# Reciprocal norms by way of DRAM, and a new order of the first tiles, in a two-layer hybrid decoder trunk

## The chip, the cores and the metric

The kernel runs on one core of one Trainium2 chip. The metric is the device time of one execution in microseconds, taken as the median of several runs; a profiled execution of the same program gives the trace. All times below are microseconds unless they say otherwise.

## The reference

A residual stream of 528 tokens (16 meta tokens and 512 of the sequence) with d = 1024 passes two layers. Each is one sub-layer with two token mixers side by side:

```
h = RMSNorm(x)
u, z, c_q, c_kv, k_rope, z_mla, g_pool, g_mla = split(h @ W_in)
y_pool = (pool_mix(u) * silu(z)) @ W_pool_up
y_mla  = (mla(c_q, c_kv, k_rope) * silu(z_mla)) @ W_mla_up
x = x + (sigmoid(g_pool) * y_pool + sigmoid(g_mla) * y_mla) @ W_out
```

pool_mix takes running means over windows of 2, 4, 8 and 16 tokens in four channel groups and multiplies each by a matrix of its own. mla is attention with 8 heads: a query latent of 768 and a key-value latent of 256 channels are normed (RMSNorm) and projected up, queries and keys are normed again, a part of each is rotated by position, and the attention is causal. What matters here are two of the norms: the RMSNorm of x, and that of the key-value latent.

## The kernel before

**Layout.** Channels lie on the 128 partitions and tokens along the free dimension. x is held as eight slices of 128 channels. Every large product is done as three fp32r products (L179 to L182): each operand is split into a high and a low part, and hi·hi, hi·lo and lo·hi are added up in PSUM. A slice of x becomes its hi and lo part in split_h (L329); a weight block of 128 by 512 is loaded by SP into one of three raw buffers, copied to its high part by ScalarE (L175), and VectorE subtracts to get the low part (L176).

**The norms come after the products.** h is not divided by its norm ahead of the product with W_in; the scale is put on when a result is taken out of PSUM. For that the kernel needs 1/rms per token, repeated on all 128 partitions: self.inv (tag rinv) for x, and self.cinv for the key-value latent. norm_sums (L340) makes them in each layer. It sums the squares (L338 for x, L407 for the latent) with matmuls against ones (L348), copies the sums out (L355), transposes them so that tokens lie on partitions (L360, L361), and VectorE takes the reciprocal root by Newton steps (L283 to L290) in the small tile ny, 128 x 2 x 5. Then the way back begins. ny is split into a high and a low part in a tile of 170 columns (L372 to L378). rows() (L387) transposes it with five matmuls to four rows over the tokens, and ScalarE copies them to kinv (L394, L395). spread() (L273) multiplies kinv by a matrix of ones and zeros, two matmuls for each of the two results, which leaves a row on all partitions; ScalarE copies it out (L277). The values v take the reciprocal norm straight from ny, per partition (L582, L583).

**The order.** plan is a list of products (Gemm objects), and stream() (L187) is a generator that emits them in that order, weight loads four blocks ahead. The code in go() (L977) draws from it by step(), by upto(name), which runs until a product is done, and by fill_now(ns), which emits products worth so many nanoseconds; between these stands the other work: norm sums, mixing stages, heads. Within that, a scheduler orders each engine's instructions. Accumulators of these products come from four PSUM banks (mm) with one bank per half of the tokens, so that a product whose evacuation is late holds up the second product behind it.

**The start of the plan.** ckv0 and ckv1 (key-value latent), three of the six query-latent tiles cq0 to cq2, then u0, k0, u1, the rotary key kr, k1, u2, k2, u3, k3 (pooling input and keys by turns), cq3, v, the gates zp with the group products y, cq4 and cq5 among them, and then the queries. The evacuation of u, kr, the keys, zp and the later gates reads self.inv or self.cinv; that of ckv and cq doesn't. The sine and cosine tables (L292) come after u0, mixing stage 3 after cq3.

**The start of the kernel.** Ten matmuls on a tile of ones (L138) run while the first loads are under way. The first weight block is loaded on ScalarE's queue into the tile later used as rinv; on SP follow the gains gn, the slices of x (1, 1, 2, 2, 2), three raw blocks between them, the constants cst and the positions, all without a wait. In layer 0 go() emits split_h for the eight slices with four steps of the stream between, then ckv1, then the squares of the slices.

The existing precedent of a way through DRAM is that of the keys' norms: kdr is written by one DMA (L685) and read back as broadcasts (L694).

Of the kernel before, what the change touches and what calls it, by code (L numbers as in the profile page):

```python
# [54 lines left out]
LAG = 2000.0  # L55
BATCH = 8
SPL = 240
WARM = 10


def cut(v, bits):
# [10 lines left out]
def trunk(ctx, tc, xT, pos, win, wkr, wqb, wkb, wvb, wgr, wpu, wmu, wout, gains, const, yT):  # L72
# [26 lines left out]
    def mmt():  # L99
        return pp.tile([P, 512], F32, tag="mm", name=nm("mm"), bufs=4)  # L100
# [19 lines left out]
    early.append(fetch(win[0, MT_CKV, :, 0:512], 512, slot("rinv"), act))  # L120
    sp.dma_start(gn, gains)
    for k0, k1, m, c in ((0, 1, 1, 0), (1, 2, None, 0), (2, 4, 0, 1), (4, 6, 1, 1), (6, 8, None, 0)):
        sp.dma_start(xb[:, k0:k1, :T], xT[:, k0:k1, :])
        if m is not None:
            early.append(fetch(win[0, MT_CKV + m, :, 512 * c:512 * c + 512], 512, rawt(), sp))
    xt = [xb[:, k] for k in range(8)]
    sp.dma_start(cst, const)
# [4 lines left out]
    sp.dma_start(posb[:, :T], pos.partition_broadcast(P))  # L132
    ident = cst[:, C_ID:C_ID + P]
    ones = cp.tile([P, P], F32, name="ones")
    dve.memset(ones, 1.0)
# [2 lines left out]
        pe.matmul(wps[:, 0:P], ones, ones, start=True, stop=True)  # L138
    maskw = cp.tile([P, 512], BF16, name="maskw")
    gp.memset(maskw[:, :512 - P], 0.0)  # L140
    dve.tensor_copy(maskw[:, 512 - P:], cst[:, C_MASK:C_MASK + P])
    kinv = cp.tile([34, T], F32R, name="kinv")
    sel = cp.tile([64, 2], F32R, name="sel")
    gp.memset(sel.bitcast(F32), 0.0)
    for i in range(2):
        gp.memset(sel[32 * i:32 * i + 2, i:i + 1].bitcast(F32), 1.0)
    identr = cp.tile([P, P], F32R, name="identr")
    dve.tensor_copy(identr, ident)
# [30 lines left out]
    def mm3(out, wh, wl, xh, xl, start, stop):  # L179
        pe.matmul(out, wh, xh, start=start, stop=False)  # L180
        pe.matmul(out, wh, xl, start=False, stop=False)  # L181
        pe.matmul(out, wl, xh, start=False, stop=stop)  # L182

    plan = []
    done = set()

# [77 lines left out]
    def fill_now(ns):  # L264
        end = clk[0] + ns
        while clk[0] < end and step():
            pass
# [5 lines left out]
    def spread(dst, i):  # L273
        for a, b in FULL:
            ps = mmt()[:, :b - a]
            pe.matmul(ps, sel[0:34, i:i + 1].to_broadcast([34, P]), kinv[:, a:b], start=True, stop=True)
            act.activation(dst[:, a:b], ps, AF.Copy)  # L277

    def behind(ins, other):
        tc.add_manual_dep(ins.ins, other.ins.name,  # L280
                          mybir.DependencyInfo(mybir.DependencyClass.Sync, mybir.DependencyReason.DATA))
# [22 lines left out]
        dve.tensor_scalar(tcos, tcos, -2.0, 1.0, op0=ALU.mult, op1=ALU.add)  # L304

    scr = dp.tile([P, 8, SEQ], F32, name="scr")
    kdr = [[dp.tile([4, T], F32, name=f"kdr{l}{s}") for s in range(2)] for l in range(DEPTH)]

    hbuf = [(slot(f"hh{k}", F32R), slot(f"hl{k}", F32R)) for k in range(8)]

    class Layer:
        def __init__(self, l):
            self.l, self.last = l, l == DEPTH - 1
            self.XS = XTOK if self.last else FULL
            self.x0 = NM if self.last else 0
            self.xt = xt if l == 0 else [None] * 8
            self.hs, self.us, self.zps = hbuf, [None] * 4, [None] * 4
            self.cs, self.cqs, self.ys, self.am = [None] * 2, [None] * 6, [None] * 4, [None] * 8
            self.kn, self.qn, self.zms, self.ogs = [None] * 4, [None] * 4, [None] * 4, [None] * 4
            self.qr, self.qf = [None] * 2, [None] * 2  # L320
            self.gms, self.mg, self.xr, self.vw = [None] * 8, [None] * 8, [None] * 8, []
            self.csq, self.xsq = [None] * 2, [None] * 8
            self.sq, self.nsq, self.asq = [], [0, 0], 0
            self.st = self.acc = self.inv = self.cinv = self.kraw = self.kp = None
# [4 lines left out]
        def split_h(self, k):  # L329
            gk, x = self.g(G_H + k), self.xt[k]  # L330
            hh, hl = self.hs[k]
            act.activation(hh[:, :T], x[:, :T], AF.Copy, scale=gk)
            dve.scalar_tensor_tensor(out=hl[:, :T], in0=x[:, :T], scalar=gk, in1=hh[:, :T].bitcast(F32),
                                     op0=ALU.mult, op1=ALU.subtract)

        def square_x(self, k):
            self.xsq[k] = slot(f"cq{4 + k}" if k < 4 else f"q{k}")
            act.activation(self.xsq[k][:, :T], self.xt[k][:, :T], AF.Square)  # L338

        def norm_sums(self):  # L340
            fill_now(2600)
            ps = [mmt(), mmt()]
            for t, r, start, stop in [(self.xsq[k], 0, k == 0, k == 7) for k in range(6)] + [
                    (self.csq[0], 32, True, False), (self.xsq[6], 0, False, False),
                    (self.xsq[7], 0, False, True), (self.csq[1], 32, False, True)]:
                for s, (a, b) in enumerate(FULL):
                    r_ = r + 64 * s
                    mm = pe.matmul(ps[s][r_:r_ + 32, :HALF], ones[:, 0:32], t[:, a:b], start=start, stop=stop,  # L348
                                   tile_position=(0, r_))
                    if t is not self.csq[1]:  # L350
# [20 lines left out]
            w = tmp()  # L371
            gp.memset(w[:, 0:170], 0.0)  # L372
            v = w[:, 0:170].rearrange("p (j c) -> p j c", c=34)
            nv = ny.rearrange("p a j -> p j a")
            nh = sm.tile([P, 5, 2], F32R, tag="nh", name=nm("nh"))
            dve.tensor_copy(nh, nv)
            dve.tensor_copy(v[:, :, 0:33:32], nh.bitcast(F32))
            dve.tensor_sub(v[:, :, 1:34:32], nv, nh.bitcast(F32))  # L378
            fill_now(8200)
            self.rows(v, 34, kinv)  # L380
            self.inv, self.cinv = slot("rinv"), slot("cq9")
            fill_now(1300)
            spread(self.inv, 0)
            spread(self.cinv, 1)
            self.st = [sct(), sct()]

        def rows(self, v, n, out):  # L387
# [523 lines left out]
        def register(self, nxt):  # L911
# [14 lines left out]
            def kk(p):  # L926
                add(f"k{p}", wkb[l, p], 256, evac=self.ev_k(p), xs=cs, segs=FULL)

            for m in range(3):
                cq(m)  # L930
            for m in range(4):
                add(f"u{m}", wi(MT_U + m), D, evac=self.ev_u(m), xs=hs, segs=FULL)
# [6 lines left out]
            def y(m):  # L939
                add(f"y{m}", wgr[l, m], P, evac=self.ev_y(m), xs=lambda: [self.ys[m]], segs=XS)  # L940

            cq(3)
            add("v", wvb[l], 1024, body=self.v_body)
            zp(0)
            zp(1)
# [2 lines left out]
            y(1)  # L948
            zp(3)
            y(2)  # L950
            cq(4)
            y(3)
            cq(5)
            for r in range(2):
                add(f"qr{r}", wqb[l, r], 768, evac=self.ev_qr(r), xs=lambda: self.cqs, segs=XS)
            for p in range(4):
# [20 lines left out]
        def go(self, nxt):  # L977
            l = self.l
            up = lambda name: upto((l, name))
            if l == 0:  # L980
                for k in range(8):
                    if k in (0, 1, 3, 5):
                        step()
                    self.split_h(k)
            up("ckv1")
            if l == 0:
                for k in range(8):
                    self.square_x(k)
            self.norm_sums()
            up("u0")  # L990
            if l == 0:
                tables()
            up("u1")
# [1 line left out]
            self.mix(1)  # L995
            up("u3")
            self.mix(2)
            up("cq3")
            self.mix(3)
            up("qr1")  # L1000
            for s, (a, b) in enumerate(FULL):
# [109 lines left out]
```

## Time and profile before

| | us |
|---|---|
| median of three runs | 802.42 (802.06 to 803.46) |
| profiled execution | 803.0 |
| its span in the trace | 801.2 |

The page of the profile lists busy time per engine, the chain of work that ended last, and groups of instructions by line. In a timeline row stand the start, the length, the engine, the line, the operation with its tiles and shapes, the count, and in brackets the idle time ahead of it with what ended it. A matmul's length is longer than its distance to the next, since matmuls overlap; what one costs is read from start to start. Every fp32 matmul leaves several records, every fp32r product of 264 columns one. In the window view each row gives the stretch, its length, then busy time and count for each engine, the clock that TensorE was granted, and the DMA engines' busy share and rate. A row of landing times gives the size in KB and the median time from issue to landing.

### The profile page before, as it was taken

How to read it: one execution, taken by the hardware profiler on the slowest of the kernel's cores; microseconds unless marked ns; L12 is line 12 of the kernel's file. 1: busy time of each engine (PE TensorE's matmuls, PEld its weight loads, DVE VectorE, ACT ScalarE, POOL GpSimd, SP SyncE). 2: the span in 40 equal slices, each digit the busy share in tenths (PEclk: the TensorE clock that was granted, in tenths of full speed). 3: DMA queues.
4: the chain of work that ended last, by engine and by line, in shares of the span. 5: the costliest groups of instructions: out<-in, count | busy, mean ns of one | idle time of the engine just before them, and what ended most of it. 6: DMA issues, size and time to landing. Idle time of an engine off the chain costs nothing.

```text
span 801.2 us, 14644 instructions
## 1 busy us (share of the span) xinstructions
PE 793.5 (99%) x5343; PEld 715.1 (89%) x5343; DVE 527.8 (66%) x1139; ACT 417.0 (52%) x946; POOL 196.2 (24%) x266
## 2 busy tenths in 40 slices
PE   9999999999999999999999999999999999999998
PEld 8889999999999999999997897877788888887887
DVE  5568767437689887685354686665467889664942
ACT  7455645545556665543254456445455666644421
POOL 1024404103433322142000164032024333410600
PEclk9999999999999999999999999999999999999999
DMA  6222233324222222224642222324242322222272
GB/s 240 73 64 96 73 100 91 109 83 140 86 87 87 78 69 67 83 89 143 181 142 73 73 87 86 98 81 119 85 157 90 101 84 79 68 78 69 92 227 102
DMA packets 48872, 80.71 MB, mean 101 GB/s; under 512 B 5904, under 2 KB 14480, under 8 KB 48800
## 3 DMA queue, kind: packets, MB, share of 16 engines
q1 hardware_dynamic: 48656, 79.52, 32.3%
q8 instruction: 42, 0.69, 0.4%
q14 instruction: 30, 0.25, 0.1%
q10 hardware_dynamic: 144, 0.26, 0.1%
HBM read 73.40 MB, written 4.23 MB: 97 GB/s over the span
## 4 chain that ended last, share of the span: by engine, by line
PE 95%; DMA 2%; ACT 1%; DVE 1%; issue 0%; POOL 0%; SPq 0%; ACTq 0%; POOLq 0%
PE mm L180 28%; PE mm L182 27%; PE mm L181 27%; PE mm L798 2%; PE S L180 2%; PE S L181 2%; PE S L182 2%; PE o L804 1%; PE o L803 1%; PE mm L348 1%; PE S L457 1%; DMA raw<-wmu 1%; DMA xb<-xT 1%; DMA bc<-kdr 1%; PE mm L415 0%
## 5 line engine op out<-in xcount | busy, mean ns | idle before, releaser
L180 PE MATMUL mm<-hh,whi 128*128 128x264 f32 (+2 forms) x1096 | 346.3, 318 | 0.2 <-ACT racc L812 0.2
L181 PE MATMUL mm<-hl,whi 128*128 128x264 f32 (+2 forms) x1096 | 343.5, 314 | 0.0
L182 PE MATMUL mm<-hh,wlo 128*128 128x264 f32 (+2 forms) x1096 | 342.2, 315 | 0.0
L176 DVE TENSOR_TENSOR wlo<-raw,whi 128x512 fp32r<-128x512 f32 (+2 forms) x251 | 186.5, 747 | 120.1 <-ACT whi L175 112.6
L175 ACT ACTIVATE whi<-raw 128x512 fp32r<-128x512 f32 (+2 forms) x251 | 150.3, 602 | 185.9 <-PE mm L181 131.5
L180 PEld LDWEIGHTS mm<-hh,whi 128*128 128x128 f32 x1096 | 205.7, 188 | 13.5 <-ACT racc L812 0.5
L181 PEld LDWEIGHTS mm<-hl,whi 128*128 128x128 f32 x1096 | 206.2, 188 | 12.2 <-issue 0.4
L182 PEld LDWEIGHTS mm<-hh,wlo 128*128 128x128 f32 x1096 | 205.1, 188 | 12.7 <-issue 0.4
L704 POOL TENSOR_TENSOR tmp<-kp,bc 64x528 f32<-64x528 f32 x16 | 24.5, 1531 | 113.5 <-DMA bc<-kdr 78.2
L535 POOL TENSOR_TENSOR racc<-racc,tmp 128x264 f32<-128x264 f32 (+1 forms) x15 | 14.1, 942 | 143.5 <-ACT tmp L534 143.4
L776 POOL TENSOR_TENSOR pm<-pa,rs 128x16 f32<-128x16 f32 x32 | 11.6, 361 | 145.5 <-DVE rs L771 140.7
L886 POOL TENSOR_TENSOR tmp<-tmp,xb 128x264 f32<-128x264 f32 (+1 forms) x24 | 27.0, 1145 | 59.1 <-DVE tmp L884 33.7
L732 DVE CUSTOM_DVE_ANT_0 S<-S,maskw,nqs 128x272 f32<-128x272 f32 (+4 forms) x80 | 38.4, 498 | 1.6 <-PE S L182 1.2
L739 ACT ACTIVATE cq<-S,bia 128x400 f32<-128x400 f32 (+2 forms) x48 | 24.6, 516 | 21.5 <-DVE bia L766 11.6
L180 PE MATMUL mm<-u,whi 128*128 128x264 f32 (+1 forms) x108 | 35.3, 327 | 0.0
L182 PE MATMUL mm<-cq,wlo 128*128 128x264 f32 (+1 forms) x108 | 34.8, 323 | 0.0
L182 PE MATMUL mm<-u,wlo 128*128 128x264 f32 (+1 forms) x108 | 34.8, 322 | 0.0
L181 PE MATMUL mm<-cq,whi 128*128 128x264 f32 (+1 forms) x108 | 34.8, 322 | 0.0
L180 PE MATMUL mm<-cq,whi 128*128 128x264 f32 (+1 forms) x108 | 34.7, 322 | 0.0
L271 DVE TENSOR_TENSOR tl<-mm,th 128x512 fp32r<-128x512 f32 (+1 forms) x64 | 29.3, 481 | 6.8 <-ACT th L270 5.8
L778 POOL TENSOR_TENSOR cq<-cq,rs 128x384 f32<-128x384 f32 (+1 forms) x32 | 32.8, 1025 | 0.0
L180 PE MATMUL mm<-q,whi 128*128 128x264 f32 (+1 forms) x96 | 30.0, 324 | 1.0 <-ACT whi L175 0.5
(262 smaller groups left out, 1380.0 us busy)
## 6 DMA issues: line engine op xcount, KB each, us to landing
raw<-win SPq DMA_DIRECT2D x143, 256.0 KB, 2.6
raw<-wout SPq DMA_DIRECT2D x32, 256.0 KB, 3.1
bc<-kdr SPq DMA_DIRECT2D x16, 264.0 KB, 3.6
raw<-wpu SPq DMA_DIRECT2D x16, 256.0 KB, 2.7
raw<-wmu SPq DMA_DIRECT2D x16, 256.0 KB, 2.6
raw<-wqb SPq DMA_DIRECT2D x12, 256.0 KB, 2.7
tmp<-xT SPq DMA_DIRECT2D x16, 132.0 KB, 2.9
tmp<-scr SPq DMA_DIRECT2D x7, 256.0 KB, 4.7
```

Of the source, the lines that this page charges most:

```text
L175: act.activation(hi[:, :n], raw[:, :n], AF.Copy)
L176: dve.tensor_sub(lo[:, :n], raw[:, :n], hi[:, :n].bitcast(F32))
L180: pe.matmul(out, wh, xh, start=start, stop=False)
L181: pe.matmul(out, wh, xl, start=False, stop=False)
L182: pe.matmul(out, wl, xh, start=False, stop=stop)
L271: dve.tensor_sub(lo[:, a:b], src, hi[:, a:b].bitcast(F32))
L704: gp.tensor_mul(kf[r0:r0 + 64, :], self.kp[r0:r0 + 64, :], bc[r0:r0 + 64, :])
L732: dve.tensor_tensor_reduce(out=sv, in0=sv, in1=mask, scale=nqs[:, i, h:h + 1], scalar=3e38, op0=ALU.add, op1=ALU.min, accum_out=bia[:, c:c ...
L739: act.activation(pv, sv, AF.Exp, scale=-1.0, bias=bia[:, i:i + 1], accum_out=rs[:, c:c + 1])
L778: gp.tensor_mul(pt[i][:, NM:], pt[i][:, NM:], rs[:, i:i + 1].to_broadcast([P, n - NM]))
L798: pe.transpose(tr[:, P * (i - j):P * (i - j + 1)], pt[i][:, NM + P * j:NM + P * (j + 1)], ident)
L886: gp.tensor_add(t[:, :b - a], t[:, :b - a], self.am[m][:, a:b])
```

## The change

- **Norms.** The high-low split, rows() and spread() are no longer called for these norms, and kinv and sel are gone. ny is written to two DRAM rows by four DMAs on SP per layer: for each of the two norms one of 128 x 4 single elements, and one for the 16 meta tokens. After a stretch of products worth RET = 12500 nanoseconds, two DMAs on SP read each row back, broadcast to all partitions, into rinv and into q1 (before: cq9). These reads wait for the latest lo·hi product emitted up to there.
- **Order of the plan.** Five query-latent tiles come after ckv1 instead of three; cq3 before v and cq4 after y2 are gone from there, and cq5 comes after y2.
- **Other work.** In layer 0 the tables come right after norm_sums, in both layers mixing stage 3 comes after k3.
- **Start.** Five loads go first: the first weight block (ScalarE's queue), then gn, x0, one raw block and x1 on SP. All other early loads wait until the first weight block has landed. Eight warm-up matmuls instead of ten. The first slice is split in two halves of the tokens, and the square of slice k in layer 0 waits for the split of slice k + 3 (at most 7).

```
-WARM = 10
+RET = 12500.0
+WARM = 8
...
+    early.append(slot("rinv"))
+    first = act.dma_start(early[0][:, 0:512], win[0, MT_CKV, :, 0:512])
     sp.dma_start(gn, gains)
...
+    sp.dma_start(xb[:, 0, :T], xT[:, 0, :])
+    early.append(fetch(win[0, MT_CKV + 1, :, 0:512], 512, rawt(), sp))
+    sp.dma_start(xb[:, 1, :T], xT[:, 1, :])
...
+    def other_loads(made):
+        for k, m in ((2, 0), (4, 1), (6, None)):
+            ins = sp.dma_start(xb[:, k:k + 2, :T], xT[:, k:k + 2, :])
+            behind(ins, made)
+            if m is not None:
+                raw = rawt()
+                behind(sp.dma_start(raw, win[0, MT_CKV + m, :, 512:1024]), made)
+                early.append(raw)
+        behind(sp.dma_start(cst, const), made)
+        behind(sp.dma_start(posb[:, :T], pos.partition_broadcast(P)), made)
...
-        pe.matmul(out, wl, xh, start=False, stop=stop)
+        newest[0] = pe.matmul(out, wl, xh, start=False, stop=stop)
...
+            for a, b in FULL if (self.l, k) == (0, 0) else [(0, T)]:
+                made = act.activation(hh[:, a:b], x[:, a:b], AF.Copy, scale=gk)
+                self.made[k] = self.made[k] or made
...
+            made = act.activation(self.xsq[k][:, :T], self.xt[k][:, :T], AF.Square)
+            if self.l == 0:
+                behind(made, self.made[min(k + 3, 7)])
...
-            fill_now(8200)
-            self.rows(v, 34, kinv)
-            self.inv, self.cinv = slot("rinv"), slot("cq9")
-            fill_now(1300)
-            spread(self.inv, 0)
-            spread(self.cinv, 1)
+            self.inv, self.cinv = slot("rinv"), slot("q1")
+            for i, d in enumerate((self.inv, self.cinv)):
+                row = ndr[self.l][i]
+                sp.dma_start(row[0, NM:T].rearrange("(j p) -> p j", p=P), ny[:, i, 0:4])
+                sp.dma_start(row[0, 0:NM].rearrange("(p j) -> p j", j=1), ny[0:NM, i, 4:5])
+            fill_now(RET)
+            for i, d in enumerate((self.inv, self.cinv)):
+                behind(sp.dma_start(d[:, 0:T], ndr[self.l][i].partition_broadcast(P)), newest[0])
...
-            for m in range(3):
+            for m in range(5):
                 cq(m)
...
-            cq(3)
             add("v", wvb[l], 1024, body=self.v_body)
...
-            cq(4)
+            cq(5)
             y(3)
-            cq(5)
...
             self.norm_sums()
-            up("u0")
             if l == 0:
                 tables()
...
-            up("cq3")
+            up("k3")
             self.mix(3)
```

More of the change, by code (lines that the diff above doesn't have):

```diff
@@ L118, in rawt @@
         return wp.tile([P, 512], F32, tag="raw", name=nm("raw"), bufs=3)
-    early.append(fetch(win[0, MT_CKV, :, 0:512], 512, slot("rinv"), act))
+    early.append(slot("rinv"))
+    first = act.dma_start(early[0][:, 0:512], win[0, MT_CKV, :, 0:512])
     sp.dma_start(gn, gains)
[L122 to L125, printed above, removed]
+    sp.dma_start(xb[:, 0, :T], xT[:, 0, :])
+    early.append(fetch(win[0, MT_CKV + 1, :, 0:512], 512, rawt(), sp))
+    sp.dma_start(xb[:, 1, :T], xT[:, 1, :])
     xt = [xb[:, k] for k in range(8)]
-    sp.dma_start(cst, const)
     warm = cp.tile([P, 1], F32, name="warm")
@@ L131, in trunk @@
     posb = slot("u3", I32)
-    sp.dma_start(posb[:, :T], pos.partition_broadcast(P))
     ident = cst[:, C_ID:C_ID + P]
@@ L140, in trunk @@
     gp.memset(maskw[:, :512 - P], 0.0)
[L141 to L146, printed above, removed]
-    identr = cp.tile([P, P], F32R, name="identr")
-    dve.tensor_copy(identr, ident)
+    identr = cp.tile([P, P], F32R, name="identr")
+    def other_loads(made):
[8 more added lines that the diff above has]
+        behind(sp.dma_start(posb[:, :T], pos.partition_broadcast(P)), made)
+        dve.tensor_copy(maskw[:, 512 - P:], cst[:, C_MASK:C_MASK + P])
+        dve.tensor_copy(identr, ident)
     tcos = cp.tile([P, T], F32, name="tcos")
@@ L181, in mm3 @@
         pe.matmul(out, wh, xl, start=False, stop=False)
-        pe.matmul(out, wl, xh, start=False, stop=stop)
+        newest[0] = pe.matmul(out, wl, xh, start=False, stop=stop)
+    newest = [None]
     plan = []
@@ L271, in split @@
         dve.tensor_sub(lo[:, a:b], src, hi[:, a:b].bitcast(F32))
[L273 to L277, printed above, removed]
     def behind(ins, other):
@@ L306, in trunk @@
     scr = dp.tile([P, 8, SEQ], F32, name="scr")
+    ndr = [[dp.tile([1, T], F32, name=f"ndr{l}{i}") for i in range(2)] for l in range(DEPTH)]
     kdr = [[dp.tile([4, T], F32, name=f"kdr{l}{s}") for s in range(2)] for l in range(DEPTH)]
@@ L321, in __init__ @@
             self.gms, self.mg, self.xr, self.vw = [None] * 8, [None] * 8, [None] * 8, []
+            self.made = [None] * 8
             self.csq, self.xsq = [None] * 2, [None] * 8
@@ L331, in split_h @@
             hh, hl = self.hs[k]
-            act.activation(hh[:, :T], x[:, :T], AF.Copy, scale=gk)
-            dve.scalar_tensor_tensor(out=hl[:, :T], in0=x[:, :T], scalar=gk, in1=hh[:, :T].bitcast(F32),
-                                     op0=ALU.mult, op1=ALU.subtract)
+            for a, b in FULL if (self.l, k) == (0, 0) else [(0, T)]:
+                made = act.activation(hh[:, a:b], x[:, a:b], AF.Copy, scale=gk)
+                self.made[k] = self.made[k] or made
+                dve.scalar_tensor_tensor(out=hl[:, a:b], in0=x[:, a:b], scalar=gk, in1=hh[:, a:b].bitcast(F32),
+                                         op0=ALU.mult, op1=ALU.subtract)
         def square_x(self, k):
             self.xsq[k] = slot(f"cq{4 + k}" if k < 4 else f"q{k}")
-            act.activation(self.xsq[k][:, :T], self.xt[k][:, :T], AF.Square)
+            made = act.activation(self.xsq[k][:, :T], self.xt[k][:, :T], AF.Square)
+            if self.l == 0:
+                behind(made, self.made[min(k + 3, 7)])
         def norm_sums(self):
@@ L370, in norm_sums @@
             newton(ny, na, nt)
[L371 to L378, printed above, removed]
-            fill_now(8200)
-            self.rows(v, 34, kinv)
-            self.inv, self.cinv = slot("rinv"), slot("cq9")
-            fill_now(1300)
-            spread(self.inv, 0)
-            spread(self.cinv, 1)
+            self.inv, self.cinv = slot("rinv"), slot("q1")
[6 more added lines that the diff above has]
+                behind(sp.dma_start(d[:, 0:T], ndr[self.l][i].partition_broadcast(P)), newest[0])
             self.st = [sct(), sct()]
@@ L984, in go @@
                     self.split_h(k)
+                    if k == 0:
+                        other_loads(first)
             up("ckv1")
```

## The prediction

> **What bounds the kernel now.** I read the page's head and busy times first, then the chain of work that ended last, then TensorE's waits.
>
> ```profile
> span 801.2 us, 14644 instructions
> ...
> PE 793.5 (99%) x5343; PEld 715.1 (89%) x5343; DVE 527.8 (66%) x1139; ACT 417.0 (52%) x946; POOL 196.2 (24%) x266
> ...
> PE 95%; DMA 2%; ACT 1%; DVE 1%; issue 0%; POOL 0%; SPq 0%; ACTq 0%; POOLq 0%
> ```
> ```profile
> PE mm L276 <- ACT rinv L277: 0.5, 1, 0.5
> ...
> PE S L180 <- ACT hh L332: 0.4, 1, 0.4
> ...
> PE mm L180 <- DVE vt L583: 0.2, 1, 0.2
> ```
>
> TensorE is busy for 99% of the span and carries 95% of the chain; no single wait listed here is over half a microsecond. So an edit pays in three ways only: it removes matmuls, it lets TensorE start sooner, or it costs a new wait. VectorE (66%), ScalarE (52%) and the queues matter where they make TensorE wait. The profiled execution took 803.0, that is 1.8 around the span of 801.2; the median of the runs is 802.42, so I take a saving as it stands on the profiled execution and set it off from the median.
>
> **Part 1: the removed matmuls.** TensorE's timeline around them, layer 0 and then layer 1:
>
> ```profile
> 40.74 0.19 PE L389 MATMUL mm<-cst,tmp 16*34 16x16 f32 x1
> 40.85 0.50 PE L391 MATMUL mm<-cst,tmp 128*34 128x128 f32 x3
> ...
> 41.22 0.37 PE L180 MATMUL mm<-hh,whi 128*128 128x264 f32 x1
> ...
> 42.49 0.63 PE L276 MATMUL mm<-kinv,sel 34*128 34x264 f32 x3
> 43.60 0.38 PE L276 MATMUL mm<-kinv,sel 34*128 34x264 f32 x1 [0.48 <-ACT rinv L277]
> 43.91 0.39 PE L180 MATMUL mm<-hh,whi 128*128 128x264 f32 x1
> ```
> ```profile
> 446.72 0.19 PE L389 MATMUL mm<-cst,tmp 16*34 16x16 f32 x1
> ...
> 447.21 0.37 PE L182 MATMUL mm<-hh,wlo 128*128 128x264 f32 x1
> 447.42 0.29 PE L180 MATMUL mm<-hh,whi 128*128 128x264 f32 x1
> ...
> 450.10 0.28 PE L181 MATMUL mm<-hl,whi 128*128 128x264 f32 x1
> 450.32 0.51 PE L276 MATMUL mm<-kinv,sel 34*128 34x264 f32 x2
> 450.75 0.39 PE L182 MATMUL mm<-hh,wlo 128*128 128x264 f32 x1
> ...
> 451.80 0.51 PE L276 MATMUL mm<-kinv,sel 34*128 34x264 f32 x2
> 452.24 0.39 PE L180 MATMUL mm<-kh,whi 128*128 128x264 f32 x1
> ```
>
> Matmuls overlap, so the cost of a group is from its start to the start of the next weight product. Layer 0: the five transposes (L389 to L392) 41.22 − 40.74 = 0.48; the four spreading products 43.91 − 42.49 = 1.42, in which lies the wait of 0.48 on ScalarE's copy of rinv. Layer 1: 0.49, then 0.43 and 0.44. The sum is 0.48 + 1.42 + 0.49 + 0.43 + 0.44 = **3.26**. Nothing on TensorE takes its place, so in a stage where it never rests this is a saving on the path. With it go, per layer, six copies on ScalarE (L277, L394, L395), three small VectorE operations and a memset on GpSimd, off the path but for the wait of 0.48.
>
> **Part 2: the new route through DRAM.** Its price is not on TensorE unless the two tiles come late. The nearest rows: the last product of ny (its next reader, L376), the existing round trip of the keys' norms, and the landing times of three kinds of loads (KB each, microseconds from issue).
>
> ```profile
> L376 DVE CAST nh<-ny x2: 157/160/164, 37.7 to 444.1; 128x10 fp32r<-128x10 f32 x2
> ```
> ```profile
> 177.03 1.72 DMA kdr<-tmp
> 178.77 4.78 DMA bc<-kdr
> ```
> ```profile
> raw<-win SPq DMA_DIRECT2D x143, 256.0 KB, 2.6
> ...
> bc<-kdr SPq DMA_DIRECT2D x16, 264.0 KB, 3.6
> ```
> ```profile
> gn<-gains SPq DMA_DIRECT2D x1, 24.0 KB, 2.6
> ```
>
> ny is ready at 37.7 (layer 0) and 444.1 (layer 1). Four writes go out, two of them 512 single elements each; then SP waits for a named matmul and issues the two reads. A read of the same size lands in 3.6 at the median, and 4.78 on the chain: I take 4.8. A write of four rows took 1.72; gn with its 128 pieces took 2.6, and four times that for 512 pieces is 10.4. So a pair of writes takes 3.4 to 21 if one follows the other; 2.6 for each of the large ones is nearest, with the small ones beside them: I take 6.
>
> When is the result needed? The cadence in the layer 1 rows is 22 products from 447.42 to 450.10, 0.122 each. In layer 0 the reads are released 26 products later than the old transposes stood: 40.74 + 26 × 0.122 = 43.9. u0's evacuation now comes after the five query tiles; u1 needs u0's accumulators back 139 products after the release, at 43.9 + 17.0 = 60.9. From 37.7 that leaves 23.2, of which the read takes 4.8: the writes may take 18.4 before TensorE stalls. In layer 1 the same count (17 products of 0.122 back from 446.72, 24 of 512 columns forward, at an estimated 0.122 × 512/264 = 0.236) gives a release near 450.3 and the need at 450.3 + 24 × 0.236 + 60 × 0.122 = 463.3; 463.3 − 444.1 − 4.8 = 14.4 for the writes. At 6 both are covered: **0**. At 21 it is 2.6 + 6.6, some +9. On SP the four writes and the wait of the reads for their matmul stand ahead of weight loads. The stream keeps four weight slices ahead of TensorE, each worth 24 products or 2.9, 11.7 in all; the wait lasts from 37.7 to 43.9, and a load behind it takes 2.6, together 8.8. So TensorE has weights, with 2.9 to spare in layer 0 and about as much in layer 1 (444.1 to 450.3); beyond that every microsecond that the writes hold the queue is a stall, which D below prices with the rest.
>
> By the Trainium skill's "DMA: Bandwidth & Descriptors", "Rules for kernel authors", an access with a strided last dimension becomes one descriptor per element, which speaks against these writes; no run here shows one yet, and the sum above does not use it.
>
> **Part 3: the start.**
>
> ```profile
> 1.05 4.64 PE L138 MATMUL wps<-ones 128*128 128x128 f32 x20 [1.05 <-DVE na L662]
> 5.34 0.79 PE L180 MATMUL S<-hh,whi 128*128 128x264 f32 x2
> ...
> 6.61 0.38 PE L181 MATMUL S<-hl,whi 128*128 128x264 f32 x1
> 6.83 0.28 PE L182 MATMUL S<-hh,wlo 128*128 128x264 f32 x1
> 6.95 0.28 PE L180 MATMUL mm<-hh,whi 128*128 128x264 f32 x1
> ...
> 7.96 0.51 PE L180 MATMUL S<-hh,whi 128*128 128x264 f32 x2 [0.37 <-ACT hh L332]
> ...
> 9.85 0.41 PE L180 MATMUL S<-hh,whi 128*128 128x264 f32 x2
> ```
> ```profile
> 4.42 0.73 ACT L332 ACTIVATE hh<-xb,gn 128x528 fp32r<-128x528 f32 x1
> ...
> 22.62 0.37 ACT L407 ACTIVATE q<-mm 128x264 f32<-128x264 f32 x1
> ```
> ```profile
> 2.12 5.04 DMA xb<-xT
> 7.17 0.74 ACT hh L332
> ```
>
> Up to 6.83 the products start 0.22 apart (6.61 to 6.83), after it 0.12 (6.83 to 6.95). The first needs hh0, which ScalarE writes from 4.42 in 0.73; a half takes 0.37 by the row of 264 columns, so the first product comes 0.36 sooner, at 5.0. The second slice waits for x1, which the chain shows from its issue to 7.16. Five loads now have the DMA engines alone until the first has landed, so x1 should land near 6 (its bytes are the same, its competitors gone; between 5.5 and 7.2, no gain), and hh1 is then ready before TensorE has done its 12 products on slice 0 (two tiles, two halves, three products). From 5.0, eight products at 0.22 reach the clock's change at 6.8, four more at 0.122 end at 7.3, twelve for slice 1 end at 8.8; with 0.3 for the other loads, now issued some microseconds later, the third slice starts at 9.15 where it was 9.85. Taken: **−0.8**, between −1.5 (nothing lost, both gains kept) and +0.3 (the later loads late). The squares move behind later slices on ScalarE; their cover is the weight products up to the sums L348, whose margin is near nothing, so up to +0.5 stands against it and is within that range.
>
> **Part 4: the moves.** Tables, tiles and the fourth mixing stage keep all their instructions. In the windows of VectorE and GpSimd (columns: length, PE, PEld, DVE, ACT, POOL, clock, DMA):
>
> ```profile
> 44.00:61.00 17.00, 17.00 (x153) 15.81 (x154) 12.70 (x28) 8.29 (x17) 5.13 (x5) 1.00 0.26 76
> 61.00:74.00 13.00, 13.00 (x114) 12.23 (x114) 12.36 (x28) 8.11 (x20) 5.98 (x7) 1.00 0.25 84
> 74.00:92.00 18.00, 18.00 (x123) 16.73 (x123) 12.12 (x26) 10.31 (x22) 8.85 (x9) 1.00 0.24 75
> ```
>
> VectorE is at 95% in the middle one. cq3, 48 products or 5.9 us, used to lie between k3 and v, and now comes before u0: v arrives 5.9 sooner against the same VectorE backlog. Over all three it works 37.2 of 48, so there is room; but the wait on vt L583 (0.2) shows that v can catch it. Zero to +1 per layer, taken as +0.1 in all, nearest to the 0.2 row.
>
> **Sum:** −3.26 − 0.8 + 0.1 = −4.0: 803.0 becomes 799.0, and 802.42 becomes **798.5**.
>
> **Rivals.**
> *B, the clock opens later.* The warm-up leaves two records per matmul, 20 from 1.05 to 5.34, so 0.214 each; with eight matmuls it ends at 1.05 + 16 × 0.214 = 4.5, half a microsecond before the first product. If the count starts over at 5.0 and takes as long as before (6.83 − 1.05 = 5.8), products stay 0.22 apart until 10.8: 26 of them by then, where before it was 24 at 9.85 and 8 more at 0.122. Six are missing: 6 × 0.122 = +0.7 instead of −0.8, 1.5 more than the forecast, **800.0**. For it: TensorE now has a gap in its warm-up. Against it: the gap is a tenth of that stretch. The Trainium skill's "TensorE: Matmul & The Clock Gate", "What's actually happening", has a free-running window of some 3.4 us that must be busy; by it the next chance after 6.8 would be 10.2, an estimate close to the one above. The trace agrees with two cadences, and does not show what a short gap does.
> *C, nothing gained at the start and v caught by VectorE.* 0 instead of −0.8 and +1 for the vt and L348 waits: −3.26 + 1.0, about **800.2 to 802**.
> *D, slower: the small writes.* If a pair takes longer than 18.4 (layer 0) or 14.4 (layer 1), all beyond is a stall. At 21 the stalls are 2.6 + 6.6 = 9.2 by Part 2: 798.5 + 9.2 = **807.7**. It decides for slower (above 804.0) from 5.5 of stalls, that is from a pair of 19.2: 0.8 in layer 0 and 4.8 in layer 1. For it: 512 pieces of four bytes have no row here. Against it: 128 pieces landed in 2.6 with issue. That the tiles do not return before they are needed is this same case.
> *E.* The start gains all of 1.5 and more: under 797.2.
>
> **How the numbers follow.** Forecast 0.45 (own range 797.2 to 799.6), B 0.27, C 0.13, D 0.10, E 0.05. Within 0.2%, 1.6 us, is about what a measurement here can tell from no change. Faster (below 800.8): 0.45 + 0.27 + 0.05 and 0.03 of C, 0.80; the same: the rest of C, 0.10; slower: D, 0.10. The range 797.0 to 801.3 leaves out D, E and part of C, 0.20.
>
> **What would show it.** No idle time of TensorE on rinv's readers, u0's evacuation or the banks behind it, in both layers (Part 2); the write's landing well under 14. The first product near 5.0, the third slice near 9.15, the cadence of 0.12 from 6.8 (Part 3) and not from 10 (B). No wait at v over 0.2 (Part 4). Sum of start-to-start savings after the norms 1.9 in layer 0 and 1.36 in layer 1. The forecast is wrong if a pair of writes takes over 14, or if TensorE waits for x1 as before.

## The result and the profile after

| | before | changed |
|---|---|---|
| median of 20 runs | 802.54 (801.84 to 803.81) | 804.16 (801.96 to 806.42) |
| profiled execution | 803.0 | 803.88 |
| its span | 801.2 | 802.1 |

The ratio is 1.0022, with a 95% interval of 1.0015 to 1.0028: slower by a little, where 798.5 and faster was forecast. The changed kernel's runs also spread more than twice as far.

The page of the changed kernel (head, busy times, chain), and then TensorE's waits:

```profile
span 802.1 us, 14590 instructions
...
PE 790.6 (99%) x5321; PEld 712.6 (89%) x5321; DVE 528.1 (66%) x1134; ACT 413.0 (51%) x935; POOL 196.8 (25%) x261
...
PE 90%; DMA 4%; DVE 3%; issue 1%; ACT 1%; POOL 1%; SPq 0%; DVEq 0%; ACTq 0%; POOLq 0%
```
```profile
PE mm L186 <- DVE vt L584: 2.8, 1, 2.8
PE mm L186 <- DVE u L477: 1.6, 1, 1.6
```

TensorE is busy 2.9 less than before, as meant, and the wait on rinv's copy is gone. But the chain has 90% of TensorE instead of 95%, and the rest went to DMA and VectorE: there are two long waits that before did not have, both in layer 0, where u0 leaves PSUM (L477) and where v does (L584). In layer 1, with the same order of products, TensorE waits at neither. TensorE's timeline around them:

```profile
60.27 0.28 PE L188 MATMUL mm<-kh,wlo 128*128 128x264 f32 x1
62.19 0.36 PE L186 MATMUL mm<-hh,whi 128*128 128x264 f32 x1 [1.64 <-DVE u L477]
```
```profile
93.20 0.40 PE L188 MATMUL mm<-whi,kl 128*128 128x512 f32 x1
96.41 0.66 PE L186 MATMUL mm<-whi,pa 128*128 128x512 f32 x1 [2.80 <-DVE vt L584]
96.86 0.63 PE L187 MATMUL mm<-wlo,pa 128*128 128x512 f32 x1
97.29 0.63 PE L188 MATMUL mm<-whi,pa 128*128 128x512 f32 x1
97.72 0.42 PE L186 MATMUL mm<-hh,whi 128*128 128x264 f32 x1
```

From start to start, less the product itself, the waits cost 1.80 and 2.97. There is a third loss, which is no wait: after 96.41 the products of 512 columns start 0.43 to 0.45 apart instead of 0.23. The window view of the same stretch (PEclk stands behind POOL's busy time) shows why:

```profile
92.00:96.00 4.00, 1.60 (x7) 0.96 (x6) 3.29 (x6) 2.62 (x7) 2.05 (x2) 1.00 0.20 68
96.00:100.00 4.00, 3.60 (x14) 3.29 (x15) 3.58 (x11) 2.24 (x5) 0.00 (x0) 0.57 0.01 4
```

The granted clock is 0.57 on average from 96 to 100. At half clock the three products and the ten of 264 columns behind them took 1.31 + 2.20 (to 99.92) where 0.69 + 1.22 is their time, a loss of 1.60.

Where the time went, from the timelines of the profiles: the first norm-sum product and the first score product (S<-kh,qhl) of each layer, and the end of TensorE's work. The first row is absolute, the others are differences to it.

| | norm sums, layer 0 | scores, layer 0 | norm sums, layer 1 | scores, layer 1 | end |
|---|---|---|---|---|---|
| before | 24.96 | 186.20 | 429.04 | 587.64 | 797.96 |
| changed | -0.40 | +4.11 | +4.09 | +1.68 | +1.12 |

At the norm sums the changed kernel is 0.40 ahead in this profile. Layer 0 loses 4.51 between the norm sums and the scores, in spite of the removed products. Layer 1 gains 2.41.

### The profile page after: what moved, and what is told of

The parts are those of the page before. It is cut to its first block, busy times and chain, and to the rows that moved or that the text cites. A ratio compares the mean times of both kernels' runs of the same rounds, so it can differ in the third digit from the quotient of the medians.

```text
span 802.1 us, 14590 instructions
## 1 busy us (share of the span) xinstructions
PE 790.6 (99%) x5321; PEld 712.6 (89%) x5321; DVE 528.1 (66%) x1134; ACT 413.0 (51%) x935; POOL 196.8 (25%) x261
## 4 chain that ended last, share of the span: by engine, by line
PE 90%; DMA 4%; DVE 3%; issue 1%; ACT 1%; POOL 1%; SPq 0%; DVEq 0%; ACTq 0%; POOLq 0%
PE mm L186 26%; PE mm L187 26%; PE mm L188 26%; PE mm L799 2%; PE S L187 2%; PE S L188 2%; PE S L186 1%; PE o L805 1%; PE o L804 1%; DMA raw<-win 1%; PE mm L355 1%; PE S L458 1%; DVE wlo L182 1%; DMA xb<-xT 1%; DMA bc<-kdr 1%
## 5 line engine op out<-in xcount | busy, mean ns | idle before, releaser
L188 PEld LDWEIGHTS mm<-hh,wlo 128*128 128x128 f32 x1096 | 205.7, 188 | 12.6 <-issue 0.4
L277 ACT ACTIVATE th<-mm 128x512 fp32r<-128x512 f32 (+1 forms) x64 | 25.4, 433 | 10.6 <-PE mm L799 10.4
```

What stands on the lines that cost most here:

```text
L188: newest[0] = pe.matmul(out, wl, xh, start=False, stop=stop)
```

## The experiments

The reasons to be told apart: **W**, the writes of single elements hold up the loads behind them, and VectorE falls behind; **V**, the order, with v directly behind k3 and mixing stage 3 ahead of v's evacuation, stalls by itself; and whether the half clock comes of the idle time. All ratios are to the kernel before, run beside it.

### The writes on another queue

```
-                sp.dma_start(row[0, NM:T]...
-                sp.dma_start(row[0, 0:NM]...
+                act.dma_start(row[0, NM:T]...
+                act.dma_start(row[0, 0:NM]...
```

> The changed kernel, with the four writes of the norms issued on ScalarE's queue instead of SP's. Theory W (the single-element writes hold up the weight loads queued behind them on SP: 8.8 us to landing instead of 2.6, VectorE idles 3.4 us and its backlog comes up as TensorE's waits of 1.6 at u0 and 2.8 at v): with the weights on a queue of their own they land in about 3 again, both waits shrink by the idle time, and the time is 798.5 to 800.5, faster than before by 2 to 4. Rival S (the 16 DMA engines are shared, so the small pieces slow the loads whatever queue they are in): loads still land in 7 or more and the time stays at 803 to 805. Rival V (the order, with v directly behind k3 and mixing stage 3 ahead of v's evacuation on VectorE, is what stalls): the loads land in time, but a wait of over 2 at v stays, 802.5 to 804.

803.11, ratio 1.0014 (1.0004 to 1.0023). DMA issues between 36 and 50, in the changed kernel and then here (KB each, time to landing):

```profile
raw<-win SPq DMA_DIRECT2D x3, 256.0 KB, 8.8
...
q<-ndr SPq DMA_DIRECT2D x1, 264.0 KB, 6.9
...
ndr<-ny SPq DMA_DIRECT2D x2, 2.0 KB, 7.7
ndr<-ny SPq DMA_DIRECT2D x2, 0.1 KB, 7.8
```
```profile
raw<-win SPq DMA_DIRECT2D x3, 256.0 KB, 10.0
...
ndr<-ny ACTq DMA_DIRECT2D x2, 2.0 KB, 10.0
ndr<-ny ACTq DMA_DIRECT2D x2, 0.1 KB, 12.4
```

Loads on SP's queue land no sooner when the writes are on ScalarE's. So it is not the place in a queue: rival S is borne out as far as that goes, loads and small pieces hold each other up in something that both queues share. What that is, this run does not show.

### Mixing stage 3 behind v

```
-            up("k3")
+            up("v")
             self.mix(3)
```

> The changed kernel, with mixing stage 3 emitted behind v instead of ahead of it. Rival V (the order): VectorE reaches the evacuation of v's third and fourth bank some 2 to 3 us sooner, the wait of 2.8 at v falls under 0.5, and the half clock of 3.4 us behind it goes too; the wait of 1.6 at u0 stays; 804.2 - 2.5 - 1.7 = about 800. Theory W alone (VectorE is behind because it idled): the backlog is still there, v still waits over 1, and the time falls by at most 2, to 802 to 804.

802.52, ratio 0.9999 (0.9990 to 1.0008), some 1.8 faster than the changed kernel by the two ratios, less than half of what V expected. TensorE's waits in it:

```profile
PE mm L186 <- DVE u L477: 1.7, 1, 1.7
...
PE mm L186 <- DVE tmp L514: 0.8, 1, 0.8
...
PE mm L186 <- DVE tmp L506: 0.4, 1, 0.4
```

The wait at v shrank to under 0.4. But the products y3, which need mixing stage 3, now wait 0.4 (L506), and a product behind them waits 0.8 for the evacuation of y (L514). A half clock of 3.4 came behind these two pieces. VectorE's backlog was moved on, not removed.

### The order alone

```
-            for m in range(3):
+            for m in range(5):
                 cq(m)
...
-            cq(3)
             add("v", ...)
...
-            up("u0")
             if l == 0:
                 tables()
...
-            up("cq3")
+            up("k3")
             self.mix(3)
```
(and cq5 behind y2, as in the change)

> The kernel before with the new order alone: five query-latent tiles first, cq5 after y2, tables right after the norm sums, mixing stage 3 after k3; norms still by transposes and spreading products, old start. Rival V: v stalls by 2 or more in layer 0, with a stretch of half clock in some runs, and the time is 804 to 807, slower than before. Theory W: without the writes VectorE does not idle for weights at 45 to 49, waits at v stay under 0.7, and the time is within 1 of before, 802 to 803.5.

808.68, ratio 1.0077 (1.0064 to 1.0091): more than V expected. TensorE's longest waits in it:

```profile
PE mm L180 <- DVE vt L583: 2.8, 1, 2.8
PE mm L276 <- ACT rinv L277: 1.5, 2, 0.8
```

No single-element write, and the same wait of 2.8 at v. The half clock lasted 6.8 in this profile. W is not needed for the larger wait. That wait is again in layer 0 alone.

### Whole rows

```
...
+            fill_now(8200)
+            t = tmp()
+            self.rows(v, 33, t[0:33, 0:T])
+            sp.dma_start(ndr[self.l], t[0:33:32, 0:T])
...
```
(in place of the four writes; v here is the small tile with one column per norm)

> The changed kernel, but the small tile of reciprocal norms is turned by five transposes on TensorE as before, copied out by ScalarE and written by one DMA of two whole rows per layer; the broadcast reads stay. It adds 0.48 a layer on TensorE, 0.97. Theory W: the write lands in about 2 as that of the keys' norms did, weight loads land in 2.6, the waits at u0 and v mostly go: 798.5 + 1 = 799.5, between 798.5 and 801. Rival V: the wait at v stays over 2 and the time is 803 to 805.

803.19, ratio 1.0007 (0.9996 to 1.0018). The weight loads are back to 2.6 (the trace has the landing of one of the four) and the wait at u0 is gone, but the wait at v is as long as ever; its DMA issues between 36 and 50, then TensorE's longest wait:

```profile
raw<-win SPq DMA_DIRECT2D x4, 256.0 KB, 2.6
```
```profile
PE mm L186 <- DVE vt L588: 2.8, 1, 2.8
```

So W explains u0's wait, and the order explains v's, in layer 0. But the order is not enough: in the four profiles with five tiles first and mixing stage 3 ahead of v (the changed kernel, the writes on another queue, the order alone, the whole rows) v waits 2.8 in layer 0 and not at all in layer 1, which has the same order. What layer 0 has besides are the sine and cosine tables, ten operations and some 6.4 of VectorE's time in the changed kernel (43.47 to 57.87), and 528 tokens in operations that have 512 in layer 1. Whether v would still wait without the tables was not tried.

### Start alone, route alone

The new start on the kernel before; and the new route of the norms on it, with the old order and start, its reads released after products worth 9500 nanoseconds instead of 12500.

> The kernel before with the new start alone (five loads first, eight warm-up matmuls, the first slice in halves, squares behind later splits). The prediction's Part 3: -0.8, between -1.5 and +0.3; from the profile of the changed kernel, where the norm sums begin at 24.57 instead of 24.96, I now expect -0.4: about 801.9. Rival (the clock opens later by up to one window of 3.4): +0.7. Whichever holds, no new wait behind 30 us.

801.06, ratio 0.9996 (0.9987 to 1.0004): a gain, if any, of about 0.3. In the ten profiles that have the new start the norm sums begin 0.26 to 0.97 earlier than in that of before; but in the route alone, which has the old start, they begin 0.42 earlier too.

> The kernel before with the new route of the norms alone (single-element writes, broadcast reads, released 9.5 us of products behind the norms), old order and start. The removed matmuls give -3.3. Theory W now adds: the tiles land near 50 where u0's evacuation began at 49 and the weight loads behind the writes are 6 late, so TensorE waits 1 to 4 at u1 in layer 0 and 0 to 4 in layer 1, and v, with cq3 ahead of it, less than 1: between 800 and 806. Rival V (the order is the only cost, the writes are free): 799.

811.24, ratio 1.0125 (1.0112 to 1.0138), dearer than the range. TensorE's longest wait in the route alone, and the windows behind its two parts:

```profile
PE mm L175 <- DVE u L467: 10.4, 2, 5.9
```
```profile
52.50:57.00 4.50, 3.71 (x19) 3.74 (x20) 4.47 (x9) 1.36 (x3) 1.40 (x1) 0.62 0.22 62
...
459.00:466.00 7.00, 4.62 (x21) 4.65 (x22) 3.87 (x8) 2.51 (x6) 1.44 (x1) 0.51 0.50 154
```

The two layers wait 4.5 and 5.9 for u0, and behind both waits the clock is halved (0.62 and 0.51 in these windows). Without the two query tiles brought forward the round trip has no cover; with them v, in layer 0, loses its own.

### Four tiles first

```
-            for m in range(5):
+            for m in range(4):
                 cq(m)
...
+            cq(4)
             add("v", ...)
...
-            up("k3")
+            up("cq4")
             self.mix(3)
```

Once with the change's writes, once with whole rows:

> The changed kernel with four query-latent tiles first, cq4 between k3 and v again, and mixing stage 3 behind cq4. Order theory V: with 5.9 us of products that ask little of VectorE between k3 and v, the wait at v falls from 2.8 to under 0.7 and the half clock goes; 804 - 2.5 - 1.7 = 799.8. But the norms come 5.9 us of products earlier to be needed, so the wait at u0 (1.6) may grow by up to 5.9: if the single-element writes bound it, 801 to 805.

> The same order, with the norms turned by TensorE and written as two whole rows. The tiles land near 49 and u0's evacuation is wanted near 49 + 5.9, so no wait at u0; v under 0.7; no half clock. 802.3 - 3.3 + 1.0 (transposes) - 0.4 (start) = 799.6, between 798.5 and 800.8. If the order theory is wrong, over 802.

802.91, ratio 1.0021 (1.0012 to 1.0030), and **798.22, ratio 0.9966** (0.9954 to 0.9979). With the single elements u0 waits in both layers, 1.5 and 2.1, and behind the second the clock is halved (0.50 in the window); v waits 0.2:

```profile
PE mm L186 <- DVE u L477: 3.6, 2, 2.1
...
PE mm L186 <- DVE vt L584: 0.2, 1, 0.2
```
```profile
458.90:462.20 3.30, 3.30 (x17) 3.30 (x16) 1.72 (x4) 2.74 (x7) 0.29 (x1) 0.50 0.50 159
```

With rows the wait at u0 is gone as well, and that at v is 0.2. The order theory holds for layer 0: with one query tile between k3 and v, and mixing stage 3 behind it, the wait of 2.8 is gone. The 0.2 is in layer 1, as in before.

### Pieces of 16 bytes

```
-row[0, NM:T].rearrange("(j p) -> p j", p=P)
+row[0, NM:T].rearrange("(p j) -> p j", p=P)
```
(on four tiles first with the change's writes; the scales then belong to other tokens, so that this kernel serves to time the pieces and not to compute)

> The order of four tiles first, with the writes again straight from the small tile, but each partition's four values go as one piece of 16 bytes: 128 pieces a write instead of 512, the same bytes. The tokens so land in another order in the DRAM row, so the scales belong to other tokens: the work is the same, the values are not. Theory W (the number of pieces sets the price): a write lands in 2.5 to 3.5, as the gains' load of 128 pieces did in 2.6, instead of 6.5 to 8.6; the weight loads behind it land in under 4, the waits at u0 (1.5 and 2.1 with 512 pieces) go, no half clock: faster than the row writes by their transposes, about 1.0, so a ratio of 0.994 to 0.997 to the kernel before. Rival (writing from the tile to DRAM in pieces under 512 bytes is slow whatever their number): the writes still take over 6, and the time is as with 512 pieces, ratio 1.002.

796.33, ratio 0.9936 (0.9923 to 0.9950), a shade better than expected. DMA issues from 36 to 50, then the packets on the pages of the single elements and of this run:

```profile
raw<-win SPq DMA_DIRECT2D x3, 256.0 KB, 3.8
...
ndr<-ny SPq DMA_DIRECT2D x2, 2.0 KB, 1.4
ndr<-ny SPq DMA_DIRECT2D x2, 0.1 KB, 4.0
```
```profile
DMA packets 51688, 81.80 MB, mean 102 GB/s; under 512 B 8208, under 2 KB 16784, under 8 KB 51616
```
```profile
DMA packets 50152, 81.80 MB, mean 103 GB/s; under 512 B 6672, under 2 KB 15248, under 8 KB 50080
```

The 1536 small packets fewer are 4 x (512 - 128), for the four large writes of the two layers. In layer 0 the same 2 KB in 128 pieces instead of 512 land in 1.4 instead of 7.2 (four tiles with single elements), and the loads behind them in 3.8 instead of 7.2. In layer 1 the one of these writes whose landing the trace has took 3.8 instead of 6.8. That is W measured by itself: 802.91 against 796.33 beside nearly equal medians of before (801.38 and 801.50), some 6.7. The number of the pieces, their size and their place in DRAM changed together, and no run tells these apart.

### The idle time filled

```
+            if self.l == 0:
+                idle = pp.tile([P, 512], F32, tag="o", ...)
+                last = newest[0]
+                for _ in range(12):
+                    behind(pe.matmul(idle, cs[0][0][:, NM:NM + P], wv[0][0], start=True, stop=True), last)
```

> The changed kernel with twelve products of 512 columns added in layer 0 that nobody reads, behind v's last weight product, where TensorE sits idle for 2.8. They take 12 x 0.23 = 2.8, so the wait is filled and no product is delayed by much. If the idle time brings the half clock of 3.4 us behind it, that stretch goes and the time falls by about 1.7, from 1.0022 of the kernel before to about 1.000. If the half clock comes from something else, the time stays at 1.002 to 1.003.

801.28, ratio 0.9996 (0.9987 to 1.0005): 2.6 parts in a thousand under the changed kernel's ratio, some 2.1, for more work. TensorE's timeline and the window:

```profile
93.46 2.96 PE L591 MATMUL idle<-whi,kh 128*128 128x512 f32 x12
96.44 0.47 PE L186 MATMUL mm<-whi,pa 128*128 128x512 f32 x1
96.75 0.39 PE L187 MATMUL mm<-wlo,pa 128*128 128x512 f32 x1
```
```profile
96.00:100.00 4.00, 3.90 (x26) 3.06 (x25) 3.71 (x12) 2.30 (x6) 0.00 (x0) 1.00 0.01 4
```

The next product that counts starts at 96.44, as in the changed kernel (96.41), but the clock is 1.00 where it was 0.57. So here the half clock comes of the idle time.

### The pieces in the right order

Four further transposes per layer take tokens four apart, so that 16-byte pieces land where they belong:

```
+            for j in range(4):
+                pe.transpose(ps[:, 5 + j, :], sums[0:33, NM + j:T:4], ident[0:33, 0:33])
...
+                sp.dma_start(row[0, NM:T].rearrange("(p j) -> p j", p=P), ny[:, i, 5:9])
```

> The kernel with 16-byte pieces made whole: four further transposes per layer, with tokens taken four apart, put the scales on the partitions so that each partition's four values are neighbours in the DRAM row, and the Newton steps run over 18 columns instead of 10. Against the 16-byte pieces in the wrong order it adds eight small transposes in all, about 0.1 each by the 0.11 between two transposes of 128 columns, so 0.5 to 1.0: a ratio of 0.994 to 0.9955 to the kernel before, faster than the row writes (0.9966). If the strided transposes cost more, or the longer chain makes a new wait, 0.996 or more.

**798.10, ratio 0.9946** (0.9932 to 0.9959): faster than both kernels, by 4.3 than the one before. Its interval and that of the row writes overlap, and in the profiles both gain the same up to the end (4.69 and 4.72 below), so that it beats these is not shown.

| differences to before, from the profiles | norm sums, layer 0 | scores, layer 0 | norm sums, layer 1 | scores, layer 1 | end |
|---|---|---|---|---|---|
| order alone | -0.01 | +5.42 | +5.61 | +5.95 | +6.28 |
| route alone | -0.42 | +3.34 | +3.46 | +9.55 | +8.82 |
| four tiles, whole rows | -0.60 | -2.95 | -2.62 | -3.99 | -4.72 |
| four tiles, 16-byte pieces | -0.41 | -3.43 | -3.56 | -5.64 | -6.38 |
| the same in order | -0.86 | -2.82 | -2.36 | -3.95 | -4.69 |

Each row compares one profile with one. The start alone, which changes nothing behind the start, has -0.75 at the norm sums and -1.47 at the scores of layer 0, so a difference of 0.7 within a stage says little.

## Why the prediction was wrong, step by step

Two terms of the sum failed: the +0.1 for the moves (Part 4), which came to 4.57 at v, and the 0 for the new route (Part 2), which came to 1.80 at u0. The saving that stood against them was larger than forecast. Of the two signs that were to show the forecast wrong neither came (a pair of writes over 14, a wait for x1); what failed were two of the signs that were to show it right, no idle time at u0 and none over 0.2 at v.

**Part 1, the removed products: right in kind, too small in size.** I took 3.26, from the start of each group to the start of the next product. But the product ahead of a group and the one behind it are stretched too. Two rows of before show it:

```profile
446.51 0.28 PE L181 MATMUL mm<-hl,whi 128*128 128x264 f32 x1
...
450.98 0.29 PE L180 MATMUL mm<-hh,whi 128*128 128x264 f32 x1
```

From 446.51 to 447.42 pass 0.91 for two products of 0.122 and the transposes, which so cost 0.67, not 0.49; from 450.10 to 450.98 it is 0.88 − 0.24 = 0.64, not 0.43. All five places come to 4.2, 2.3 of it in layer 0 and 1.9 in layer 1. Layer 1 of the changed kernel, where nothing stalls, gains 2.41: 1.9 of removed products, and the 0.35, from start to start, that before lost at v, leave 0.16.

**Part 2, the new route: the step that failed is the cover of the loads behind the writes.** The writes of both norms took 9.2 from the first issue (36.76) to the last landing (issued at 38.19, 7.8 to landing), inside the bounds of 3.4 to 21, and the second tile had landed at 52.9 (its read issued at 45.98, 6.9 to landing), well ahead of the 60.9 at which I had TensorE need them (it stopped after 60.27). The forecast priced a pair up to 18.4 at nothing, and it cost 1.80 at 9.2. The loads behind the writes were not held back on SP, as I had it: they were issued from 38.80 on, but took 8.8 at the median instead of 2.6. The cover counted TensorE's weights alone. What it left out are the two engines that prepare them, and the wait came by way of ScalarE and VectorE:

```profile
48.12 0.63 ACT L181 ACTIVATE whi<-raw 128x512 fp32r<-128x512 f32 x1 [4.08 <-DMA raw<-win]
```
```profile
48.78 0.69 DVE L182 TENSOR_TENSOR wlo<-raw,whi 128x512 fp32r<-128x512 f32 x1 [3.41 <-ACT whi L181]
...
60.68 0.43 DVE L177 TENSOR_TENSOR raw<-raw,gn 128x256 f32<-128x256 f32 x1 [1.67 <-DMA raw<-wkr]
...
61.62 0.77 DVE L477 TENSOR_TENSOR u<-mm,rinv 128x264 f32<-128x264 f32 x2
```

VectorE stands idle 3.41 for a late weight. Late low parts give raw buffers back late, the rotary key's load is issued late, and u0's evacuation stands behind that load's scaling on VectorE, though rinv had long landed. (The next low part was late too: VectorE made it from 61.02 to 61.70, just before TensorE went on at 62.19.) Between the late weight and that load the chain also passes the tables, which before came behind u0 in the program:

```profile
38.80 9.22 DMA raw<-win
...
52.18 1.18 DVE tmp L300
...
54.72 1.28 ACT L302
...
58.64 1.95 DMA raw<-wkr
```

In layer 1, without tables, a write and the load behind it took 8.6 and 9.1, and u0 didn't wait; with whole rows u0 didn't wait in layer 0 either, tables and all. So with five tiles first it seems to take both; with four, u0 waits 2.1 in layer 1 without any tables. The Trainium skill's "DMA: Bandwidth & Descriptors", "Rules for kernel authors", which the prediction cited and left out of its sum, has one descriptor per element for such writes. The trace agrees, with 1536 packets under 512 bytes more than for the 16-byte pieces; the price, 7.2 against 1.4 for the same bytes in layer 0, is this case's own.

**Part 3, the start: its gain is not shown.** −0.40 in the profile where −0.8 was taken, −0.3 measured alone with an interval that includes no gain at all. The norm sums begin at 24.00 to 24.71 in the ten profiles with the new start and at 24.55 to 24.97 in the three with the old one, so one profile doesn't tell. The first product came at 4.97 (5.0 forecast), the third slice at 9.42 (9.15). Of rival B: the clock did not open later. In the changed kernel's profile products were 0.12 apart from 5.60, in that of four tiles with whole rows, with the same start, only from about 6.8. By the clock's records in the traces it opened between 4.35 and 6.73 with eight warm-up matmuls and between 4.53 and 6.82 with ten. So it varies from run to run, and two warm-up matmuls more or less do not decide it. In the changed kernel's profile the early clock gained little, since TensorE then stood for a weight's high part, which waited for its load:

```profile
5.72 0.28 PE L188 MATMUL S<-hh,wlo 128*128 128x264 f32 x1
6.62 0.39 PE L186 MATMUL mm<-hh,whi 128*128 128x264 f32 x1 [0.61 <-ACT whi L181]
```

**Part 4, the moves: the step that cost most.** I took +0.1, up to +1 per layer, since VectorE's work over the three windows had room. The wait was 2.97 and the half clock 1.60 more. The room was there as a sum, but not ahead of v: in before VectorE was busy 12.4 of the 13 ahead of 74, v now comes 5.9 sooner against its work, and cq3 was the stretch in which it caught up; in the changed kernel it is busy 15.8 of the 18 from 74 to 92, where it was 12.1. This holds for layer 0. In layer 1 the forecast of next to nothing came true: no wait at v, where before had its 0.2. Rival C had this mechanism, with about a third of the wait. No rival had the half clock. Added up for layer 0, 4.57 of cost at v and 1.80 at u0 against 2.3 removed make +4.07, where the stage table has +4.51.

What is not settled: what the tables, the moved tiles and the moved mixing stage each give to the wait at v was not tried apart (the tables began on VectorE at 43.47, and in before at 43.77, so their move shifted their start little); nor was the five-tile order with 16-byte pieces. Near the end the profile of before has a wait of 0.46 on a weight, which most others lack; between the scores of layer 1 and the end most rows of the tables gain 0.6 to 0.7 that goes with it, and its cause is open.

## What to carry to other kernels

A move of products is priced by what the other engines can catch up in the stretch that it takes away, not by their average load. A DMA is priced by its pieces, and by what is behind it: the late landing that hurt here was that of the weights, not of the result. And a stall of TensorE of two microseconds or more was dearer than it looked, since half clock came with it.

## What the runs showed of the hardware

- **Small pieces.** 512 pieces of 4 bytes, written from SBUF to DRAM, landed in 6.8 to 8.6 on SP's queue and in 7.4 to 12.6 on ScalarE's; 128 pieces of 16 bytes in 1.4 to 1.6 in layer 0 and, where the traces have it, 3.8 and 4.2 in layer 1. Weight loads issued between 36 and 50 next to the former took 7.2 to 9.4 at the median of each profile, on a queue of their own 10.0, next to the latter 3.8. In this window (40 slices of 0.35) the DMA engines of the changed kernel moved little for long:

```profile
DMA  5000150240000000946228370402093138999799
GB/s 222 0 0 0 1 5 0 2 4 0 0 0 0 0 0 0 88 193 129 23 18 23 18 23 6 18 12 18 18 111 41 12 141 339 421 328 282 265 372 386
```

 From about 39.2 to 41.6 they move nothing at all, though four writes and two loads are under way; what fills that time the trace doesn't show.

- **The clock.** In the profiles, idle times of TensorE of 2.1 (four tiles first), 2.8 (five-tile order) and 4.5 and 5.9 (route alone) each brought a stretch of half clock of 3.4 or 6.8; idle times of 1.5 to 1.7 at u0 brought none; 1.2 in two pieces within three microseconds once did (mixing stage 3 behind v). So the length of one idle time does not decide it alone. The Trainium skill's "TensorE: Matmul & The Clock Gate", "HAM oscillation — how this bites in real kernels", gives as its rule that no gap should be over some 3.4 us. Here 2.1 was enough, so the measurement is the stricter one.
- **A change of kind.** Around a group of fp32 products among the fp32r ones, the product ahead and the one behind each take 0.21 to 0.23 from start to start instead of 0.12 (446.51 to 446.72 and 447.21 to 447.42 in before), about 0.1 on each side beside the group's own time.
